# Values of the attention: the product with the probabilities taken once for four query blocks instead of once for two

## The chip, the cores and the metric

The kernel runs on one core of one Trainium2 chip. The metric is the device time of one execution in microseconds (us), lower is better. A core has a matrix engine (TensorE, PE in the profile, with its weight loads on a row of their own, PEld), a vector engine (VectorE, DVE), a scalar engine (ScalarE, ACT), a general engine (GpSimd, POOL) and an engine that issues transfers (SyncE, SP). Each works off a queue of its own in order; semaphores tie them together. A matrix product takes a stationary operand of 128x128 (loaded just ahead of it) and streams the columns of a moving operand past it; the result lands in an accumulation bank (PSUM) of 128 rows by 512 columns.

## The reference, cut to what matters

One layer of a streaming encoder on 1024 frames of 1024 channels: a normalised input goes through one wide projection, then attention beside a pooling branch, a gated mix, and a gated feed-forward part. The change lies in the attention alone, 8 heads of 64 channels; chunk c of 64 frames sees its own chunk and the eight before it:

```python
sc = jnp.einsum('bqhd,bkhd->bhqk', q_c, k_c) * scale + bias
sc = jnp.where(valid, sc, -1e30)
p = jax.nn.softmax(sc, axis=-1)
return jnp.einsum('bhqk,bkhd->bqhd', p, v_c)
```

## The kernel before, in words

The program is one core's instruction stream in four stages: input projection with its normalisation and pooling, attention (the stage of this change), output and mix, feed-forward. All matrix products except transposes are in a rounded 32-bit format (fp32r in the profile). Where precision asks for it, an operand is held as two such tensors, the rounded value and the rest ("hi" and "lo"); `split` (L77) makes the pair from a source: ACT casts to hi, DVE (or POOL) subtracts to get lo.

Attention works in blocks of 128 queries by 128 keys; there are 8 query blocks, and query block j sees key blocks j-4 to j, where they exist. A loop over 32 steps (head h, J) handles two query blocks, 2J and 2J+1, in each step. The parts of a step, each emitted in a later turn of the loop than the one before:

- `scores` (L836): for each of the two query blocks the products of queries and keys into a bank pair `pst` (640 columns once all five key blocks exist, as two products of 320, each for the hi and lo part of the keys), then on DVE bias and row maximum (L864), on ACT the exponential (L866), on DVE the reciprocal (L868), on POOL the scaling (L870) to the probabilities `pe`.
- `transposed` (L874): PE turns each 128x128 block of `pe` (L891) into one of two banks `tp`; ACT and DVE split it (L78) into `pth` and `ptl`. There are two pairs of these tiles, for even and odd J, each with 6 slots of key blocks by 256 columns, the two query blocks side by side. For J of 2 and 3 a step has ten blocks, in three fillings of a bank: 4, 2 and 4.
- `values_of` (L905): for each slot two products (hi, lo) of 256 columns (L916) with the values `vv` of one key block stationary, summed in one half of a bank `f`. The first slot holds nothing for the second query block and the last nothing for the first; those blocks of `pth` and `ptl` are zeros, set once by POOL (L962, L963). A head takes 4, 8, 12 and 12 products. After the odd J, `f` holds four query blocks: ACT and DVE add its two halves (L924, L925), and a split writes a piece of `ath` and `atl`.
- `yb_units` (L929): products of the pooling branch with its output weights (`ybp`, 512 columns each), handed out in 32 pieces of six products, by the table `NU`, one entry for each turn of the loop; they give PE something to do while the other engines are at work. After every second piece DVE multiplies the bank by a gate `sgb` (L944).

In turn i of the loop (L968), the order of emission is: scores of step i, transposes of step i-1, the `yb` pieces, values of step i-2. A scheduler then places the instructions on the engines, mostly near that order, with those that would wait put later. `tp` and `pst` have two buffers each, `f` has one bank, and `yb` has one.

Of the kernel before, what the change touches and what calls it, by code (L numbers as in the profile page):

```python
# [10 lines left out]
F32 = mybir.dt.float32  # L11
F32R = mybir.dt.float32r
# [5 lines left out]
P = 128  # L18
# [27 lines left out]
def trunk(ctx, tc, xn, xt, w_first, w_in, cols, gain_pre, bias, w_ao, w_pg, w_po, w_o, gains, w_up, w_dn, out):  # L46
    nc = tc.nc
    A, V, G = nc.scalar, nc.vector, nc.gpsimd
# [28 lines left out]
    def split(hi, lo, src, eng=None):  # L77
        return A.copy(hi, src), (eng or V).tensor_tensor(lo, src, hi.bitcast(F32), ALU.subtract)  # L78
# [287 lines left out]
    with ExitStack() as ph:  # L366
# [30 lines left out]
        for n, tag in enumerate(("T1h", "T1l", "T2h", "T2l")):  # L397
# [6 lines left out]
        q = {(i, j): raw_tile(f"xq{i}{j}").rearrange("p (k n) -> p k n", k=4)  # L404
             for j in range(2) for i in range(2)}
# [371 lines left out]
    ap_ = pool(atp, "atp", 1, side="right")  # L777
    ath = ap_.tile([P, 4, S], F32R, name="ath")
    atl = ap_.tile([P, 4, S], F32R, name="atl")

    wrp = pool(atp, "wrp", 2, side="right")

# [25 lines left out]
    with ExitStack() as ph:  # L808
# [64 lines left out]

        def transposed(J, pes):  # L874

            pth, ptl = PT[J % 2]
            fl = [t.rearrange("p s q -> p (s q)") for t in (pth, ptl)]
            (pa, na), (pb, nb) = pes
            sa, sb = 5 - na, 6 - nb
            if J == 0:  # L880
                banks = [[(pa, 0, 1, sa, 0), (pb, 0, 2, sb, 1)]]
            elif J == 1:
                banks = [[(pa, 0, 3, sa, 0)], [(pb, 0, 4, sb, 1)]]
            else:
                banks = [[(pa, 1, 4, 1, 0)], [(pa, 0, 1, 0, 0), (pb, 0, 1, 1, 1)], [(pb, 1, 4, 2, 1)]]
            for runs in banks:
                tp = psT.tile([P, 512], F32, tag="t", name="tp")
                c = 0
                for pe, b0, n, s0, a in runs:
                    for b in range(b0, b0 + n):  # L890
                        nc.tensor.transpose(tp[:, c * P:(c + 1) * P], pe[:, b * P:(b + 1) * P], ident)  # L891
                        c += 1
                if J >= 2 and len(runs) == 2:
                    moves = [(0, 2, [t[:, 0:768].rearrange("p (b q) -> p b q", b=2)[:, :, :P] for t in fl])]
                else:
                    moves, c = [], 0
                    for pe, b0, n, s0, a in runs:
                        moves.append((c, n, [t[:, s0:s0 + n, a * P:(a + 1) * P] for t in (pth, ptl)]))
                        c += n
                for c, n, (hi, lo) in moves:  # L900
                    split(hi, lo, tp[:, c * P:(c + n) * P].rearrange("p (b q) -> p b q", b=n))

        avs = {}

        def values_of(h, J):  # L905
            m, e = h // 2, h % 2
            vv = vvs[m]
            if J % 2 == 0:
                avs[h] = psf.tile([P, 512], F32, tag="f", name="f")
            f = avs[h]  # L910
            slots = [s for s in range(6) if 2 * J - 4 + s >= 0]
            fo = f[:, 256 * (J % 2):256 * (J % 2) + 256]
            for s in slots:
                kb = 2 * J - 4 + s
                for x, t in enumerate(PT[J % 2]):
                    nc.tensor.matmul(fo, vv[:, kb, e].rearrange("p a d -> p (a d)"),  # L916
                                     t[:, s], start=s == slots[0] and x == 0,
                                     stop=s == slots[-1] and x == 1)
            if J % 2 == 0:
                return  # L920
            r = slice(64 * e, 64 * e + 64)
# [32 lines left out]
        load_pair(0)  # L954
        load_yb(1)
        load_wy(2)
        PT = []
        for i in range(2):
            pth = atn.tile([P, 6, 256], F32R, name=f"pth{i}", bufs=1)
            ptl = atn.tile([P, 6, 256], F32R, name=f"ptl{i}", bufs=1)  # L960
            for t in (pth, ptl):
                G.memset(t[:, 0, 128:256].bitcast(F32), 0.0)  # L962
                G.memset(t[:, 5, 0:128].bitcast(F32), 0.0)  # L963
            PT.append((pth, ptl))
        units = yb_units()
        NU = [2, 2, 0, 1, 0, 1, 1, 2] + [0, 1, 1, 2] * 5 + [0, 1, 1, 1, 1, 1]
        steps = [(h, J) for h in range(H) for J in range(4)]
        for i in range(len(steps) + 2):  # L968
            if 0 < i < len(steps):
# [590 lines left out]
```

## Time and profile before

| what | value |
| --- | --- |
| median of 3 runs (1236.58 to 1236.9) | 1236.82 us |
| span of the profiled execution, first to last instruction | 1234.9 us |
| PE busy, share of the span | 1225.3 us, 99% |
| DVE busy | 949.6 us, 77% |
| ACT busy | 667.2 us, 54% |
| POOL busy | 211.0 us, 17% |
| granted PE clock, mean of the core | 0.998 |

The profiled execution has no time of its own besides its span; the span is 1.9 us under the median of the runs. A busy engine is one that has an instruction in flight. Matmuls overlap, so the duration of one in a row (389 ns for 512 columns) is longer than what it costs in a stream of them; the distance from one start to the next is what counts.

### The profile page before, as it was taken

How to read it: one execution, taken by the hardware profiler on the slowest of the kernel's cores; microseconds unless marked ns; L12 is line 12 of the kernel's file. 1: busy time of each engine (PE TensorE's matmuls, PEld its weight loads, DVE VectorE, ACT ScalarE, POOL GpSimd, SP SyncE). 2: the span in 40 equal slices, each digit the busy share in tenths (PEclk: the TensorE clock that was granted, in tenths of full speed). 3: DMA queues.
4: the chain of work that ended last, by engine and by line, in shares of the span. 5: the costliest groups of instructions: out<-in, count | busy, mean ns of one | idle time of the engine just before them, and what ended most of it. 6: DMA issues, size and time to landing. Idle time of an engine off the chain costs nothing.

```text
span 1234.9 us, 16242 instructions
## 1 busy us (share of the span) xinstructions
PE 1225.3 (99%) x5743; PEld 1020.9 (83%) x5743; DVE 949.6 (77%) x1551; ACT 667.2 (54%) x1171; POOL 211.0 (17%) x183
## 2 busy tenths in 40 slices
PE   9999999999999999999999999999999999999997
PEld 7888888888889987888888888888888888888886
DVE  5898677866788878756799887667666675999968
ACT  6764355555577773434546555554545455445553
POOL 0000000043254545000000112433333300000000
PEclk9999999999999999999999999999999999999999
DMA  9879245438886845322352232222132127902103
GB/s 329 333 256 350 85 147 207 154 124 264 291 276 214 264 178 207 137 86 76 113 196 111 111 145 103 71 84 102 52 102 85 61 68 255 350 18 103 34 1 137
DMA packets 63857, 193.84 MB, mean 157 GB/s; under 512 B 6048, under 2 KB 6688, under 8 KB 58656
## 3 DMA queue, kind: packets, MB, share of 16 engines
q1 hardware_dynamic: 55712, 176.55, 40.8%
q10 hardware_dynamic: 7056, 12.59, 2.7%
q0 software_dynamic: 1008, 3.67, 0.7%
q8 instruction: 45, 0.74, 0.2%
q14 instruction: 36, 0.29, 0.1%
HBM read 139.84 MB, written 52.95 MB: 156 GB/s over the span
## 4 chain that ended last, share of the span: by engine, by line
PE 92%; DVE 6%; issue 1%; DMA 0%; ACT 0%; POOL 0%; DVEq 0%; ACTq 0%
PE X_u L84 19%; PE X_i L84 12%; PE Y_u L84 10%; PE Y_i L84 9%; PE X L84 7%; PE wops L1115 7%; PE Z_u L84 4%; PE y L84 4%; PE ybp L84 4%; PE Y L84 4%; PE f L916 3%; PE tp L891 2%; PE Z_i L84 2%; PE first L466 2%; PE pst L848 1%; DVE a L1405 1%
## 5 line engine op out<-in xcount | busy, mean ns | idle before, releaser
L1239 DVE SCALAR_TENSOR_TENSOR hc<-hu,cv,hc 128x1022 f32<-128x1022 f32 (+1 forms) x88 | 115.6, 1315 | 27.7 <-ACT hc L1234 27.7
L78 ACT CAST wh_u<-s_u 128x512 fp32r<-128x512 f32 x88 | 54.4, 619 | 90.2 <-PE Y_u L84 47.7
L78 DVE TENSOR_TENSOR wl_u<-s_u,wh_u 128x512 fp32r<-128x512 f32 x88 | 62.4, 711 | 33.9 <-ACT wh_u L78 33.9
L78 ACT CAST wh_i<-s_i 128x512 fp32r<-128x512 f32 x64 | 39.8, 622 | 75.9 <-PE X_i L84 36.0
L78 ACT CAST wh_u<-wup 128x512 fp32r<-128x512 f32 x60 | 37.3, 621 | 52.0 <-PE X_u L84 27.5
L78 DVE TENSOR_TENSOR wl_i<-s_i,wh_i 128x512 fp32r<-128x512 f32 x64 | 46.2, 722 | 21.3 <-ACT wh_i L78 16.3
L1234 ACT ACTIVATE hc<-hu,cv 128x1024 f32<-128x1024 f32 x44 | 54.6, 1244 | 9.8 <-DVE hu L1183 8.9
L202 POOL TENSOR_TENSOR s_i<-win 128x512 f32<-128x512 f32 x4 | 5.9, 1481 | 257.0 <-DVE wl_i L78 246.6
L202 POOL TENSOR_TENSOR s_u<-wup 128x512 f32<-128x512 f32 x15 | 25.7, 1713 | 139.4 <-DVE wl_u L78 139.4
L78 DVE TENSOR_TENSOR ptl<-tp,pth 128x512 fp32r<-128x512 f32 (+3 forms) x80 | 42.8, 552 | 7.7 <-ACT pth L78 7.2
L866 ACT ACTIVATE pe<-sm,st 128x640 f32<-128x640 f32 (+2 forms) x64 | 44.3, 695 | 7.7 <-DVE st L864 7.5
L870 POOL TENSOR_SCALAR pe<-pe,st 128x640 f32<-128x640 f32 (+4 forms) x58 | 40.7, 705 | 44.2 <-DVE st L868 30.0
L78 ACT CAST pth<-tp 128x512 fp32r<-128x512 f32 (+3 forms) x80 | 36.3, 474 | 15.9 <-PE tp L891 11.0
L78 DVE TENSOR_TENSOR wl_u<-wup,wh_u 128x512 fp32r<-128x512 f32 x60 | 43.0, 719 | 1.2 <-ACT wh_u L78 0.5
L84 PE MATMUL ybp<-mx,wh_yb 128*128 128x512 f32 x128 | 43.3, 412 | 0.0
L1244 ACT ACTIVATE hc<-hc 128x1024 f32<-128x1024 f32 x22 | 23.4, 1062 | 36.9 <-DVE hc L1239 36.9
L864 DVE CUSTOM_DVE_ANT_0 sm<-pst,bt 128x640 f32<-128x640 f32 (+2 forms) x64 | 40.7, 651 | 3.0 <-issue 1.7
L206 POOL TENSOR_TENSOR s_u<-s_u,wup 128x512 f32<-128x512 f32 x15 | 19.4, 1291 | 102.3 <-DVE wl_u L78 99.6
L916 PE MATMUL f<-pth,vv 128*128 128x256 f32 x144 | 36.6, 286 | 0.0
L916 PE MATMUL f<-ptl,vv 128*128 128x256 f32 x144 | 36.5, 287 | 0.0
L208 POOL TENSOR_TENSOR s_u<-wup 128x512 f32<-128x512 f32 x15 | 32.2, 2144 | 23.5 <-DVE wl_u L78 23.5
L891 PE MATMUL tp<-ident,pe 128*128 128x128 f32 x240 | 35.3, 274 | 0.2
(523 smaller groups left out, 4135.7 us busy)
## 6 DMA issues: line engine op xcount, KB each, us to landing
wup<-in_w_up SPq DMA_DIRECT2D x22, 1024.0 KB, 5.0
win<-in_w_in SPq DMA_DIRECT2D x16, 1024.0 KB, 7.0
g_d<-hc SPq DMA_DIRECT2D x20, 512.0 KB, 2.6
sig_d<-d ACTq DMA_DIRECT2D x32, 256.0 KB, 2.0
a<-g_d SPq DMA_DIRECT2D x8, 1024.0 KB, 11.4
b<-in_w_dn SPq DMA_DIRECT2D x8, 1024.0 KB, 12.7
w<-in_w_in SPq DMA_DIRECT2D x12, 512.0 KB, 7.3
x<-in_xn SPq DMA_DIRECT2D x8, 512.0 KB, 8.5
```

The costliest lines, as they stand in the source:

```text
L78: return A.copy(hi, src), (eng or V).tensor_tensor(lo, src, hi.bitcast(F32), ALU.subtract)
L84: nc.tensor.matmul(ps, a[i], b[i], start=start and i == 0 and p == 0, stop=stop and i == n - 1 and p == 2, skip_group_check=True,)
L202: self.eng.tensor_tensor(self.s1, self.w21, self.w22, ALU.add)
L208: self.eng.tensor_tensor(self.s3, self.w11, self.w21, ALU.subtract)
L864: V.tensor_tensor_reduce(so, sv, bv, -1.0, 3e38, ALU.add, ALU.min, st[:, 0:1])
L866: A.activation(pe[:, :n], sm[:, :n], AF.Exp, scale=-1.0, bias=st[:, 0:1], accum_out=st[:, 1:2])
L870: (V if 4 * h + J in (0, 1, 31) else G).tensor_scalar(pe[:, :n], pe[:, :n], st[:, 2:3], 1.0, ALU.mult, ALU.mult)
L891: nc.tensor.transpose(tp[:, c * P:(c + 1) * P], pe[:, b * P:(b + 1) * P], ident)
L916: nc.tensor.matmul(fo, vv[:, kb, e].rearrange("p a d -> p (a d)"), t[:, s], start=s == slots[0] and x == 0, stop=s == slots[-1] and x == 1)
L1115: nc.tensor.matmul(ps[:, 512 * c:512 * c + 512], a[k // 4][:, k % 4, sl], wo[k][b][:, 512 * c:512 * c + 512], start=k == 0 and x == 0, sto ...
L1234: A.activation(c, hu, AF.Identity, scale=cv[:, C_CW + 88 + b:C_CW + 89 + b], bias=cv[:, C_CB + b:C_CB + b + 1])
L1239: V.scalar_tensor_tensor(c[:, n:], hu[:, :S - n], cv[:, w:w + 1], c[:, n:], ALU.mult, ALU.add)
```

## The change

The two pairs of tiles become one pair of 20 blocks of 128x128: block 5a+d holds query block a of the group of four, and key block a+d-4 counted from the group's first. An even J fills a of 0 and 1, an odd J a of 2 and 3. Blocks of one key block then lie four blocks apart, and a product takes all query blocks that see a key block, one to four of them, as a moving operand in pieces of 128 columns at that distance. Values are taken only after an odd J: 8 products after J=1 (widths 512, 384, 256 and 128 columns, hi and lo) and 16 after J=3 (each width four times), with the widest first. No zero blocks are left. In the loop, the group's values come ahead of the next step's transposes, after that turn's `yb` pieces, and `NU` hands these out one in each turn. A tile `edge` of 8 columns is placed behind `ath` and `atl` and set to zero by POOL; nothing reads it. The splits of the transposed blocks have the same count and sizes as before and write contiguous blocks.

```diff
@@ -777,6 +777,8 @@
     ath = ap_.tile([P, 4, S], F32R, name="ath")
     atl = ap_.tile([P, 4, S], F32R, name="atl")
+    edge = ap_.tile([P, 8], F32, name="edge")
+    G.memset(edge, 0.0)
...
@@ transposed @@
-            pth, ptl = PT[J % 2]
-            fl = [t.rearrange("p s q -> p (s q)") for t in (pth, ptl)]
+            k = 2 * (J % 2)
             (pa, na), (pb, nb) = pes
-            sa, sb = 5 - na, 6 - nb
+            spans = [(pa, 0, na, k, 5 - na), (pb, 0, nb, k + 1, 5 - nb)]
...
-                banks = [[(pa, 1, 4, 1, 0)], [(pa, 0, 1, 0, 0), (pb, 0, 1, 1, 1)], [(pb, 1, 4, 2, 1)]]
+                banks = [[(pa, 0, 4, k, 0)], [(pa, 4, 1, k, 4), (pb, 0, 1, k + 1, 0)], [(pb, 1, 4, k + 1, 1)]]
...
+                    at = 5 * a + d
+                    split(PT[0][:, at:at + n], PT[1][:, at:at + n],
+                          tp[:, c * P:(c + n) * P].rearrange("p (b q) -> p b q", b=n))
+                    c += n
@@ values_of @@
-            slots = [s for s in range(6) if 2 * J - 4 + s >= 0]
-            fo = f[:, 256 * (J % 2):256 * (J % 2) + 256]
-            for s in slots:
-                kb = 2 * J - 4 + s
-                for x, t in enumerate(PT[J % 2]):
-                    nc.tensor.matmul(fo, vv[:, kb, e].rearrange("p a d -> p (a d)"),
-                                     t[:, s], start=s == slots[0] and x == 0,
-                                     stop=s == slots[-1] and x == 1)
             if J % 2 == 0:
                 return
+            f = psf.tile([P, 512], F32, tag="f", name="f")
+            grid = [t.rearrange("p (a d) q -> p a d q", a=4) for t in PT]
+            slots = (4, 5, 6, 7) if J == 1 else (3, 4, 2, 5, 1, 6, 0, 7)
+            for s in slots:
+                kb = 2 * J - 6 + s
+                a0, a1 = max(0, s - 4), min(3, s)
+                for x, t in enumerate(grid):
+                    flat = t.rearrange("p a d q -> p (a d) q")
+                    at = 5 * a0 + s - a0
+                    nc.tensor.matmul(f[:, a0 * P:(a1 + 1) * P], vv[:, kb, e].rearrange("p a d -> p (a d)"),
+                                     flat[:, at:at + 4 * (a1 - a0) + 1:4],
+                                     start=s == slots[0] and x == 0, stop=s == slots[-1] and x == 1,
+                                     skip_group_check=True)
@@ -954,16 +954,9 @@
-            for t in (pth, ptl):
-                G.memset(t[:, 0, 128:256].bitcast(F32), 0.0)
-                G.memset(t[:, 5, 0:128].bitcast(F32), 0.0)
-            PT.append((pth, ptl))
+        PT = [atn.tile([P, 20, P], F32R, name=f"pt{x}", bufs=1) for x in "hl"]
         units = yb_units()
-        NU = [2, 2, 0, 1, 0, 1, 1, 2] + [0, 1, 1, 2] * 5 + [0, 1, 1, 1, 1, 1]
+        NU = [2, 2, 0, 1, 1, 1, 1, 1] + [1, 1, 1, 1] * 5 + [1, 1, 1, 1, 1, 1]
...
+            if i >= 2 and steps[i - 2][1] % 2:
+                for _ in range(NU[i]):
+                    next(units, None)
+                values_of(*steps[i - 2])
+                NU[i] = 0
             if 1 <= i <= len(steps):
                 transposed(steps[i - 1][1], pend.pop(i - 1))
...
-            if i >= 2:
-                values_of(*steps[i - 2])
```

What the scheduler makes of it shows on two engines. The first place is PE's queue in the middle of the stage, at the values of head 3 after J=1 (f is their bank, tp a bank of transposes, ybp a piece of the pooling branch, pth and ptl the hi and lo blocks). Before:

```order
L84 MATMUL ybp_3837<-mx09_2114,wl_yb3_3662 128x512
L916 MATMUL f_3844<-pth1_3034,vv1_3212 128x256
L916 MATMUL f_3844<-ptl1_3035,vv1_3212 128x256
L916 MATMUL f_3844<-pth1_3034,vv1_3212 128x256
L916 MATMUL f_3844<-ptl1_3035,vv1_3212 128x256
L916 MATMUL f_3844<-pth1_3034,vv1_3212 128x256
L891 MATMUL tp_3885<-ident_77,pe_3820 128x128 x4
L916 MATMUL f_3844<-ptl1_3035,vv1_3212 128x256
```

and in the changed kernel:

```order
L84 MATMUL ybp_3840<-mx05_1595,wl_yb4_3837 128x512
L917 MATMUL f_3847<-ptl_3031,vv1_3200 128x512
L917 MATMUL f_3847<-pth_3030,vv1_3200 128x384
L917 MATMUL f_3847<-ptl_3031,vv1_3200 128x384
L917 MATMUL f_3847<-pth_3030,vv1_3200 128x256
L917 MATMUL f_3847<-ptl_3031,vv1_3200 128x256
L917 MATMUL f_3847<-pth_3030,vv1_3200 128x128
L917 MATMUL f_3847<-ptl_3031,vv1_3200 128x128
L892 MATMUL tp_3861<-ident_77,pe_3771 128x128 x4
```

The products have become fewer and of four widths, and the next step's transposes, which stood among them, now stand behind the group.

The second place is ACT's queue at the turn from one head to the next: casts of transposed blocks, exponentials (ACTIVATE), and COPY, the first step of emptying the bank `f`. Before:

```order
L78 CAST pth_3034<-tp 128x4x128 [waits PE_49,Activation_49]
L866 ACTIVATE pe,st<-sm,st 128x384 [waits DVE_49]
L866 ACTIVATE pe,st<-sm,st 128x512 [waits DVE_49]
L78 CAST pth_3028<-tp 128x128 [waits PE_49,Activation_49]
L78 CAST pth_3028<-tp 128x2x128 [waits DVE_49]
L924 COPY sm_4035<-f 64x512 [waits PE_49]
```

and in the changed kernel:

```order
L78 CAST pth<-tp 128x512 [waits PE_49,Activation_49]
L868 ACTIVATE pe,st<-sm,st 128x512 [waits DVE_49,Activation_49]
L78 CAST pth<-tp 128x128 [waits PE_49]
L868 ACTIVATE pe,st<-sm,st 128x640 [waits DVE_49]
L78 CAST pth<-tp 128x256 [waits DVE_49,PE_49]
L924 COPY sm_3978<-f 64x512 [waits PE_49]
```

The casts of the next head's first blocks (128 and 256 columns) went from the other pair of tiles (`pth_3028`, while the values in progress read `pth_3034`) to the one pair that these values read, and the wider of the two waits for PE as well.

More of the change, by code (lines that the diff above doesn't have):

```diff
@@ L874, in transposed @@
         def transposed(J, pes):
-            pth, ptl = PT[J % 2]
-            fl = [t.rearrange("p s q -> p (s q)") for t in (pth, ptl)]
+            k = 2 * (J % 2)
             (pa, na), (pb, nb) = pes
-            sa, sb = 5 - na, 6 - nb
+            spans = [(pa, 0, na, k, 5 - na), (pb, 0, nb, k + 1, 5 - nb)]
             if J == 0:
-                banks = [[(pa, 0, 1, sa, 0), (pb, 0, 2, sb, 1)]]
+                banks = [spans]
             elif J == 1:
-                banks = [[(pa, 0, 3, sa, 0)], [(pb, 0, 4, sb, 1)]]
+                banks = [spans[:1], spans[1:]]
             else:
-                banks = [[(pa, 1, 4, 1, 0)], [(pa, 0, 1, 0, 0), (pb, 0, 1, 1, 1)], [(pb, 1, 4, 2, 1)]]
+                banks = [[(pa, 0, 4, k, 0)], [(pa, 4, 1, k, 4), (pb, 0, 1, k + 1, 0)], [(pb, 1, 4, k + 1, 1)]]
             for runs in banks:
@@ L888, in transposed @@
                 c = 0
-                for pe, b0, n, s0, a in runs:
+                for pe, b0, n, a, d in runs:
                     for b in range(b0, b0 + n):
@@ L892, in transposed @@
                         c += 1
+                c = 0
                 if J >= 2 and len(runs) == 2:
[L894 to L901, printed above, removed]
@@ L903, in trunk @@
-        avs = {}
+                    runs = [(None, 4, 2, k, 4)]
+                for pe, b0, n, a, d in runs:
+                    at = 5 * a + d
+                    split(PT[0][:, at:at + n], PT[1][:, at:at + n],
+                          tp[:, c * P:(c + n) * P].rearrange("p (b q) -> p b q", b=n))
+                    c += n
         def values_of(h, J):
             m, e = h // 2, h % 2
[L907 to L910, printed above, removed]
-            slots = [s for s in range(6) if 2 * J - 4 + s >= 0]
-            fo = f[:, 256 * (J % 2):256 * (J % 2) + 256]
-            for s in slots:
-                kb = 2 * J - 4 + s
-                for x, t in enumerate(PT[J % 2]):
-                    nc.tensor.matmul(fo, vv[:, kb, e].rearrange("p a d -> p (a d)"),
-                                     t[:, s], start=s == slots[0] and x == 0,
-                                     stop=s == slots[-1] and x == 1)
@@ L919, in values_of @@
             if J % 2 == 0:
                 return
+            vv = vvs[m]
+            f = psf.tile([P, 512], F32, tag="f", name="f")
[11 more added lines that the diff above has]
+                                     skip_group_check=True)
@@ L956, in trunk @@
         load_wy(2)
[L957 to L960, printed above, removed]
-            for t in (pth, ptl):
-                G.memset(t[:, 0, 128:256].bitcast(F32), 0.0)
-                G.memset(t[:, 5, 0:128].bitcast(F32), 0.0)
-            PT.append((pth, ptl))
+        PT = [atn.tile([P, 20, P], F32R, name=f"pt{x}", bufs=1) for x in "hl"]
         units = yb_units()
-        NU = [2, 2, 0, 1, 0, 1, 1, 2] + [0, 1, 1, 2] * 5 + [0, 1, 1, 1, 1, 1]
+        NU = [2, 2, 0, 1, 1, 1, 1, 1] + [1, 1, 1, 1] * 5 + [1, 1, 1, 1, 1, 1]
         steps = [(h, J) for h in range(H) for J in range(4)]
```

## The prediction

> **What bounds the kernel now.** I read the page first, then the share of engines in the stretch of the attention, then its groups of instructions, and last its timeline on PE, where the distance between starts gives the price of a product. The page:
>
> ```profile
> span 1234.9 us, 16242 instructions
> PE 1225.3 (99%) x5743; PEld 1020.9 (83%) x5743; DVE 949.6 (77%) x1551; ACT 667.2 (54%) x1171; POOL 211.0 (17%) x183
> PE 92%; DVE 6%; issue 1%; DMA 0%; ACT 0%; POOL 0%; DVEq 0%; ACTq 0%
> ```
>
> PE is busy for 99% of the span, and the chain that ended last lies on PE for 92%. So PE work that goes is time that goes, unless a wait takes its place. The stage, by the table of stretches, from the first scores to the last values:
>
> ```profile
> core 0: us, PE busy (x) PEld busy (x) DVE busy (x) ACT busy (x) POOL busy (x), PEclk, DMA share, GB/s
> 322.00:460.00 138.00, 137.76 (x920) 123.70 (x919) 114.38 (x319) 102.42 (x249) 66.74 (x86) 1.00 0.71 234
> ```
>
> PE is never idle there and its clock is full (1.00), but DVE has 23.6 us left of 138, ACT 35.6: the other engines follow closely. The groups on PE:
>
> ```profile
> L84 PE MATMUL ybp<-mx,wh_yb 128*128 128x512 f32 x128 | 43.3, 412 | 0.0
> L916 PE MATMUL f<-pth,vv 128*128 128x256 f32 x144 | 36.6, 286 | 0.0
> L916 PE MATMUL f<-ptl,vv 128*128 128x256 f32 x144 | 36.5, 287 | 0.0
> L891 PE MATMUL tp<-ident,pe 128*128 128x128 f32 x240 | 35.3, 274 | 0.2
> L848 PE MATMUL pst<-qk 128*128 128x320 f32 x64 | 19.1, 310 | 0.0
> ```
>
> The values are 288 products. Their mean of 286 ns is a duration with overlap, not a price. The price is on the timeline (start, duration):
>
> ```profile
> 321.88 0.28 PE L857 MATMUL pst<-qk 128*128 128x256 f32 x1
> ...
> 402.18 0.28 PE L916 MATMUL f<-pth,vv 128*128 128x256 f32 x1
> 402.30 0.60 PE L891 MATMUL tp<-ident,pe 128*128 128x128 f32 x4
> 402.66 0.37 PE L916 MATMUL f<-ptl,vv 128*128 128x256 f32 x1
> 402.86 0.28 PE L916 MATMUL f<-pth,vv 128*128 128x256 f32 x1
> ...
> 406.96 0.34 PE L857 MATMUL pst<-qk 128*128 128x384 f32 x1
> 407.13 0.34 PE L857 MATMUL pst<-kl,qk 128*128 128x384 f32 x1
> 407.31 0.39 PE L857 MATMUL pst<-qk 128*128 128x512 f32 x1
> 407.54 0.40 PE L857 MATMUL pst<-kl,qk 128*128 128x512 f32 x1
> 407.78 0.40 PE L84 MATMUL ybp<-mx,wh_yb 128*128 128x512 f32 x1
> ...
> 409.93 0.28 PE L916 MATMUL f<-pth,vv 128*128 128x256 f32 x1
> ...
> 411.32 0.31 PE L848 MATMUL pst<-qk 128*128 128x320 f32 x1
> 411.47 0.31 PE L848 MATMUL pst<-kl,qk 128*128 128x320 f32 x1
> ...
> 460.13 0.28 PE L916 MATMUL f<-ptl,vv 128*128 128x256 f32 x1
> ```
>
> Twelve products of 256 columns fill 409.93 to 411.32: 0.116 us each. 384 columns cost (407.31 - 406.96) / 2 = 0.175, 512 columns (407.78 - 407.31) / 2 = 0.235, 320 columns 0.15. Each step of 128 columns is worth about 0.059 ((0.235 - 0.116) / 2). Four transposes stand between two value products: 402.86 - 402.18 = 0.68, less two value products of 0.116, leaves 0.45, so 0.112 us for a transpose of 128 columns, almost the price of 256 columns.
>
> **The products.** Removed: 288 x 0.116 = 33.4 us. Added, for each head 3 slots of each width (one after J=1, two after J=3), hi and lo, 8 heads: 48 products each of 512, 384, 256 and 128 columns. The first three widths have rows: 48 x (0.235 + 0.175 + 0.116) = 25.2 us. The 128-column product in fp32r has none; nothing in this kernel multiplies fp32r narrower than 256. Call its price X. Then the change is 25.2 + 48 X - 33.4, zero at X = 0.171.
>
> From below: by the slope of the wider ones, 0.116 - 0.059 = 0.057. From above I take the row with four times the columns, 0.235. In between lies the row nearest in kind, the transpose: 128 columns streamed after a fresh stationary operand of 128x128, 0.112. I take 0.112, since a value product too loads a new operand every time, and something other than columns plainly holds the transpose up. That makes 48 x 0.112 = 5.4, in all 30.6 us, a gain of 2.8 us. With the ends: 27.9 (gain 5.5) and 36.5 (loss 3.1).
>
> The Trainium skill has both readings on one page, "TensorE: Matmul & The Clock Gate". In its section "Back-to-back issue gap" an isolated product costs its columns at 2.4 GHz plus 2.5 ns, 56 ns for 128 columns; by that the gain is an estimated 5.5 us. In "LDWEIGHTS (loading the stationary operand)" the load takes the operand's columns at 1.2 GHz, 107 ns for 128; by that it is an estimated 3.1. The transpose row, 0.112, agrees with the second.
>
> **The moving operand in pieces** of 128 columns, four blocks apart: no row shows such a reading, every moving operand so far is contiguous. I price it at nothing; if the jumps cost, they add to 144 wide products, and 20 ns each would eat the gain.
>
> **Transposes and splits.** 240 transposes and 80 pairs of cast and subtraction stay, in the same sizes, writing contiguous blocks instead of blocks 256 apart. Rows of before, with other work of the two engines:
>
> ```profile
> L78 DVE TENSOR_TENSOR ptl<-tp,pth 128x512 fp32r<-128x512 f32 x40 | 27.5, 688 | 4.7 <-ACT pth L78 4.2
> L866 ACT ACTIVATE pe<-sm,st 128x640 f32<-128x640 f32 x32 | 26.5, 831 | 5.4 <-DVE st L864 5.3
> L78 ACT CAST pth<-tp 128x512 fp32r<-128x512 f32 x40 | 23.1, 577 | 10.0 <-PE tp L891 9.9
> L78 DVE TENSOR_TENSOR ptl<-tp,pth 128x256 fp32r<-128x256 f32 x24 | 10.0, 417 | 2.6 <-ACT pth L78 2.6
> L78 ACT CAST pth<-tp 128x256 fp32r<-128x256 f32 x24 | 8.9, 373 | 5.2 <-DVE ptl L78 4.7 <-PE tp L891 0.6
> L944 DVE TENSOR_TENSOR sgb<-ybp,sgb 128x512 f32<-128x512 f32 x16 | 11.0, 685 | 0.5 <-PE ybp L84 0.3
> ```
>
> No change on DVE and ACT; their 23.6 and 35.6 us of room cover a small one either way.
>
> **Zero blocks and `edge`.** Eight fills go from POOL, one small one comes:
>
> ```profile
> 323.07 0.22 POOL L962 MEMSET pth<- 128x128 f32 x1
> 332.27 0.80 POOL L870 TENSOR_SCALAR pe<-pe,st 128x640 f32<-128x640 f32 x1 [6.97 <-DVE st L868]
> ```
>
> POOL waits 6.97 us for DVE afterwards, so nothing is won. `edge` moves what lies behind it by 32 bytes; nothing in the trace puts a price on an address, I take zero.
>
> **The single pair of tiles.** The casts of the next head's first blocks now wait for the running group, and behind them in ACT's queue stand an exponential, the next cast and the COPY that empties `f`; DVE's subtractions follow, and PE's next transposes need the bank that these free. But the slots are taken in the order 3, 4, 2, 5, 1, 6, 0, 7: the first blocks to be overwritten (a=0 with d=4, a=1 with d=3 and 4) are read by slots 4 and 5, done after half the group. Behind slot 5's hi product PE still has 0.175 + 4 x 0.116 + 4 x 0.112 and, by the order, two scores products of 0.15 and three transposes, 1.7 us in all, against one cast of 256 columns and one subtraction, 0.373 + 0.417 = 0.79. Covered; 0.
>
> **`yb` pieces.** The same 32, one per turn instead of 0, 1, 1, 2. Before, PE waited about once a head for a bank of transposes:
>
> ```profile
> 400.37 0.40 PE L84 MATMUL ybp<-mx,wl_yb 128*128 128x512 f32 x1
> 400.76 0.41 PE L891 MATMUL tp<-ident,pe 128*128 128x128 f32 x2
> ...
> PEld tp L891 <- issue: 2.8, 7, 0.4
> PEld tp L891 <- DVE ptl L78: 1.7, 6, 0.4
> ```
>
> Here 0.39 us lie between the starts where 0.235 do without a wait: 0.155 lost. The queue behind it is the same kind of sequence in the changed kernel, a subtraction that stands behind `sgb` (0.685) on DVE. I leave the waits as they are. After the attention the order on every engine is the same as before, so nothing else moves.
>
> Sum: -2.8 us. The span of 1234.9 becomes 1232.1; the runs' median lies 1.9 above the span, and I add that unchanged: 1236.8 - 2.8 = **1234.0 us**. A measurement of this kernel can tell about 0.2%, 2.5 us, from no change; the forecast stands just past it.
>
> **Rivals.**
>
> *The narrow products are slow.* Below 256 columns the rounded format could lose its rate, so that 128 columns cost as much as 512. For it: no such product exists in this kernel, and scores of one key block (128 columns) are computed 256 wide. Against it: the transpose's 0.112, though that is another mode. Price X = 0.235, 48 x (0.235 - 0.112) = 5.9 us more than forecast: 1239.9, slower by 3.1. It decides from X = 0.171 on.
>
> *Narrow products cost their columns.* X = 0.057: 48 x 0.055 = 2.6 us better, 1231.3. Against it the transposes. [...]
>
> *The gain is taken back as waits.* DVE keeps its 114.38 us while PE's 138 shrink, and the group of values now comes in one piece with the splits of its last bank just ahead. Two more waits of 0.155 a head are 16 x 0.155 = 2.5 us: 1236.5, no change. For it: DVE's share; against it: the order puts other products between the last transposes of a group and the products that need them.
>
> *The one pair of tiles holds the next head up.* If the casts are released only by the group's last product, PE has 0.63 us of cover (two scores products, three transposes) against cast, exponential, cast and subtraction, 0.25 + 0.831 + 0.373 + 0.417 = 1.87 (the 128-column cast, 0.25, is an estimate by the step from 512 to 256 columns): 1.24 a head, 7 turns, 8.7 us: 1242.7. It decides when the casts are released later than slot 5.
>
> **How the numbers follow.** Forecast 0.46, slow narrow products 0.25, cheap ones 0.10, waits 0.14, tiles 0.05. The forecast's own range is 1232.8 to 1235.5 (X from 0.09 to 0.14); two thirds of it lie past 0.2%. Faster: 0.31 + 0.10 = 0.41. Same: 0.15 + 0.14 + 0.05 of the slow products, which stand near their bound too, = 0.34. Slower: 0.20 + 0.05 = 0.25. The range reaches from the cheap to the slow narrow product, 1231.0 to 1240.2, and leaves out the tiles and the tails.
>
> **What would show it.** The starts of the 128-column products on the timeline: 0.11 apart (forecast), 0.06 or 0.24. 512, 384 and 256 columns at 0.235, 0.175 and 0.116 in spite of the pieces. The attention, now 321.88 to 460.13 at its last value product, ending near 457.3. Waits of weight loads for the transposes no longer than now. The forecast is wrong if a 128-column product costs over 0.17, if wide ones in pieces cost more than contiguous ones, or if the casts of the next head's first blocks show waits on PE that PE itself then waits out.

## The result, and the profile after

The changed kernel takes 1242.41 us (1239.8 to 1242.84), the kernel before 1236.9 (1236.58 to 1237.02): ratio 1.0042, 95% interval 1.0031 to 1.0053. It is slower by 5.5 us. The profiled execution took 1242.84 us, its span is 1241.1, 6.2 us above that of before.

The page of the changed kernel, with the span, the engines and the chain that ended last:

```profile
span 1241.1 us, 16085 instructions
PE 1226.8 (99%) x5647; PEld 1016.2 (82%) x5647; DVE 951.5 (77%) x1551; ACT 669.7 (54%) x1171; POOL 208.9 (17%) x176
PE 90%; DVE 8%; issue 1%; ACT 0%; DMA 0%; POOL 0%; DVEq 0%
```

It reads like the page before: 96 matmuls fewer, PE still 99% busy, and only DVE's 8% of the chain instead of 6% says that something waits longer. The products themselves did what they were meant to. The timeline of PE, at a group of values after J=1:

```profile
452.01 0.39 PE L917 MATMUL f<-ptl,vv 128*128 128x512 f32 x1
452.24 0.34 PE L917 MATMUL f<-pth,vv 128*128 128x384 f32 x1
...
452.59 0.28 PE L917 MATMUL f<-pth,vv 128*128 128x256 f32 x1
452.71 0.28 PE L917 MATMUL f<-ptl,vv 128*128 128x256 f32 x1
452.83 0.22 PE L917 MATMUL f<-pth,vv 128*128 128x128 f32 x1
452.89 0.27 PE L917 MATMUL f<-ptl,vv 128*128 128x128 f32 x1
453.00 0.92 PE L892 MATMUL tp<-ident,pe 128*128 128x128 f32 x6
```

From start to start: 0.23 us for 512 columns, 0.175 for 384 (two of them in 0.35), 0.12 for 256, in spite of the pieces; 0.06 for the first product of 128 columns and 0.11 for the next. After J=3, where four stand in a row, it is 0.06, then three times 0.11. So 48 of them cost some 4.6 us and all the value products 29.9 instead of 33.4: 3.5 us less work on TensorE. The time went up all the same: this gain got lost in the attention, and more was lost behind it.

**In the attention** the 3.5 us didn't come out. The table of stretches:

```profile
322.00:460.00 138.00, 136.30 (x817) 117.09 (x816) 114.40 (x317) 103.69 (x247) 64.34 (x79) 1.00 0.81 246
```

The stretch is 138 us long in both kernels, so 136.30 us busy against 137.76 say that TensorE's visible idle time grew by 1.46 us; in the place of the value products stand 9 `y` products more, from the stage behind. Not all idle time is visible: a product's record lasts longer than the distance to the next start (0.28 us at 0.116), so that a gap of up to 0.16 us behind a product does not show. What a head costs is better read from the same product in two heads, four heads apart. In before and in the changed kernel:

```profile
373.21 0.34 PE L857 MATMUL pst<-qk 128*128 128x384 f32 x1
440.89 0.34 PE L857 MATMUL pst<-qk 128*128 128x384 f32 x1
```

```profile
374.03 0.33 PE L859 MATMUL pst<-qk 128*128 128x384 f32 x1
441.09 0.34 PE L859 MATMUL pst<-qk 128*128 128x384 f32 x1
```

16.92 us a head became 16.77. The products' gain alone would have made it 16.5 (3.5 / 8 = 0.44 less). The view of waits (us, times, longest) shows what stands in the place of the rest:

```profile
PEld ybp L84 <- DVE sgb L944: 3.0, 9, 0.4
PEld tp L892 <- DVE ptl L78: 1.8, 4, 1.0
PEld f L917 <- ACT pth L78: 1.1, 5, 0.3
```

The first wait is new: the first product of a `yb` pair waits until VectorE has emptied the one `yb` bank of the pair before. The second is about what it was (1.7 us before), the third was 0.3.

**Behind the attention** 5.9 us are lost at one product. It is the first of the fifth `y` tile; in before:

```profile
480.43 0.39 PE L84 MATMUL y<-ath,wl_ya 128*128 128x512 f32 x1
480.84 0.47 PE L84 MATMUL y<-ath,wh_ya 128*128 128x512 f32 x1
```

and in the changed kernel:

```profile
481.18 0.40 PE L84 MATMUL y<-ath,wl_ya 128*128 128x512 f32 x1
484.88 0.76 PE L84 MATMUL y<-ath,wh_ya 128*128 128x512 f32 x1 [3.30 <-DVE ya L1030]
485.44 0.63 PE L84 MATMUL y<-atl,wh_ya 128*128 128x512 f32 x1
...
490.56 0.41 PE L84 MATMUL y<-atl,wh_ya 128*128 128x512 f32 x1
...
480.00:490.00 10.00, 6.70 (x19) 5.02 (x18) 9.25 (x8) 2.57 (x5) 4.73 (x3) 0.69 0.48 169
```

Up to the row at 481.18 the changed kernel is 0.75 us late, 0.45 of them already at the first scores product (322.33 against 321.88), behind a stage that the change leaves alone. Then 3.70 us pass where before 0.41 did: 3.29 lost. Then 13 products start 0.43 apart instead of 0.234, and the clock granted in those ten microseconds is 0.69: (490.56 - 484.88) - 13 x 0.234 = 2.6 lost. Together 6.7 us; 0.5 of them come back further on, which leaves the 6.2 of the span. The half rate did not strike every time: four of the five executions of this kernel show a granted clock of 0.996 or 0.997 and take 1242.3 to 1242.84 us, the fifth shows 0.998 and takes 1239.8.

Why VectorE answers late there is on its own timeline. Two tiles hold `y`, so the fifth needs the third emptied (L1030 here, L1034 in before). Before:

```profile
461.11 0.69 DVE L925 TENSOR_TENSOR sm<-f,sm 64x512 f32<-64x512 f32 x1 [1.86 <-ACT sm L924]
463.99 1.23 DVE L1034 TENSOR_TENSOR ya<-y,ya 128x1024 f32<-128x1024 f32 x1 [0.82 <-PE y L84]
...
479.48 1.21 DVE L1034 TENSOR_TENSOR ya<-y,ya 128x1024 f32<-128x1024 f32 x1
```

and in the changed kernel, with GpSimd's second pair of subtractions below it:

```profile
465.19 0.69 DVE L925 TENSOR_TENSOR sm<-f,sm 64x512 f32<-64x512 f32 x1 [2.80 <-ACT sm L924]
468.08 1.23 DVE L1030 TENSOR_TENSOR ya<-y,ya 128x1024 f32<-128x1024 f32 x1 [0.82 <-PE y L84]
...
471.17 1.21 DVE L1030 TENSOR_TENSOR ya<-y,ya 128x1024 f32<-128x1024 f32 x1
...
475.70 3.42 DVE L1031 TENSOR_TENSOR ya<-ya 128x1024 f32<-128x1024 f32 x1
479.80 2.13 DVE L78 TENSOR_TENSOR mix00l<-ya,mix00h 128x512 fp32r<-128x512 f32 x1 [0.69 <-ACT mix00h L78]
...
483.52 1.21 DVE L1030 TENSOR_TENSOR ya<-y,ya 128x1024 f32<-128x1024 f32 x1
484.77 1.23 DVE L1031 TENSOR_TENSOR ya<-ya 128x1024 f32<-128x1024 f32 x1
```

```profile
475.18 6.20 POOL L78 TENSOR_TENSOR wol<-wo,woh 128x1024 fp32r<-128x1024 f32 x2
```

The whole chain stands 4.1 us later (468.08 against 463.99). It starts from the last value product, which was at 460.13 and is at 464.21 now. In PE's queue 23 `y` products stand ahead of it, 9 before, and 14 x 0.234 = 3.3 us, which with the 0.75 us of lateness makes up the shift; the bank `f` is emptied behind it. From the first to the third L1030 the chain is as long as before, 15.4 us (483.52 - 468.08) against 15.5, although VectorE takes the second tile's L1030 (471.17) ahead of the first tile's `mix` subtractions now, and took it behind them before: what has changed is its start. In before the third tile was emptied at 480.69 (479.48 + 1.21), and the product that needs it started 0.15 later, as it does in the changed kernel (484.73 and 484.88). It stood 0.41 us behind its predecessor there, not 0.234: the place was waiting by some 0.18 us already, and there was no slack to take. And the chain is slow because VectorE's operations are stretched while GpSimd subtracts: L1031 takes 3.42 us at 475.70 and 1.23 at 484.77.

### The profile page after: what moved, and what is told of

Same layout as the page of the kernel before. It is cut to its first block, busy times and chain, and to the rows that moved or that the text cites. A ratio compares the mean times of both kernels' runs of the same rounds, so it can differ in the third digit from the quotient of the medians.

```text
span 1241.1 us, 16085 instructions
## 1 busy us (share of the span) xinstructions
PE 1226.8 (99%) x5647; PEld 1016.2 (82%) x5647; DVE 951.5 (77%) x1551; ACT 669.7 (54%) x1171; POOL 208.9 (17%) x176
## 4 chain that ended last, share of the span: by engine, by line
PE 90%; DVE 8%; issue 1%; ACT 0%; DMA 0%; POOL 0%; DVEq 0%
PE X_u L84 19%; PE X_i L84 12%; PE Y_u L84 10%; PE Y_i L84 9%; PE X L84 7%; PE wops L1111 7%; PE Z_u L84 4%; PE Y L84 3%; PE ybp L84 3%; PE y L84 3%; PE f L917 2%; PE tp L892 2%; PE Z_i L84 2%; PE first L466 2%; PE pst L850 1%; DVE a L1401 1%
## 5 line engine op out<-in xcount | busy, mean ns | idle before, releaser
L78 DVE TENSOR_TENSOR wl_i<-s_i,wh_i 128x512 fp32r<-128x512 f32 x64 | 44.9, 702 | 22.0 <-ACT wh_i L78 16.9
L892 PEld LDWEIGHTS tp<-ident,pe 128*128 128x128 f32 x240 | 28.2, 140 | 8.3 <-DVE ptl L78 1.8
L84 PE MATMUL Y_u<-T1h,wl_u 128*128 128x512 f32 x88 | 34.2, 389 | 0.0
```

The source lines that it names most:

```text
L84: nc.tensor.matmul(ps, a[i], b[i], start=start and i == 0 and p == 0, stop=stop and i == n - 1 and p == 2, skip_group_check=True,)
```

## The experiments

The runs below are compared with the kernel before on the same chip, 1236.6 to 1236.9 us. Where an expectation speaks of the third `y` tile that waits, it is the third that is emptied late and the fifth that waits for it.

**Without the subtractions for the low half of w_o** in `split_wo`'s calls behind the third and fifth `y` tile:

```
             if m in (2, 4):
-                split_wo(wraw[m // 2 - 1], wopa, G)
+                raw = wraw[m // 2 - 1]
+                for k in range(2):
+                    hi = wopa.tile([P, D], F32R, tag="woh", name="woh")
+                    A.copy(hi, raw[:, k * D:(k + 1) * D])
+                    wo.append((hi, hi))
```

> The changed kernel without POOL's four subtractions of the first half of w_o, right behind the attention (the hi part stands in for the lo part of that half, so half of one small correction of the mix product is left out). Nothing else moves. Theory A (the loss lies behind the attention: the last value product comes 4.1 us later, so DVE's gating chain starts 4.1 us later, runs slowly while POOL subtracts, and PE waits 3.3 us for the third bank of y and then runs 5.3 us at half clock): the gating of 475.70 takes about 1.2 us instead of 3.42, the wait falls under 0.5 us, the clock stays full, 1242.4 - 3.3 - 2.5 = 1236.6 us. Rival B (the chain is late on its own, POOL's work beside it does not matter): a wait of over 2 us and the half clock stay, 1241 us or more.

Measured: 1236.13 us, ratio 0.9995 (0.9987 to 1.0004). The 6.3 us are back. The chain still starts late, at 467.53, but reaches the third L1030 9.2 us later (476.73) instead of 15.4, and the fifth tile's first product no longer waits:

```profile
480.63 0.39 PE L84 MATMUL y<-ath,wl_ya 128*128 128x512 f32 x1
480.86 0.40 PE L84 MATMUL y<-ath,wh_ya 128*128 128x512 f32 x1
```

The same edit in the kernel before:

> The kernel before, with GpSimd's four subtractions for the first half of w_o left out (the high half is used in the place of the low one, so the last projection's result is less exact). Theory A, the subtractions cost the changed kernel 6.3 us only because its gating chain starts 4.1 us late and the third y tile then waits for VectorE: before, the same place waited 0.16 us, so this run gives 1236.7, no more than 0.3 below the kernel before. Rival, the subtractions cost either kernel their time: 1230.6, as much below the kernel before as the first experiment lay below the changed kernel.

Measured: 1235.95 us, ratio 0.9992 (0.9983 to 1.0001), 0.8 less than before, where the expectation allowed 0.3, and not the 6.3 of the changed kernel. So the subtractions have little price of their own: they cost 6 us only on top of the late chain. And with them away the two kernels stand at 1235.95 and 1236.13: the attention of the changed kernel has brought nothing.

The other way to part the two engines, with nothing left out, hands the same subtractions to VectorE, three tiles later in the program (the scheduler then ran two of the four at 468.99 and 472.94, between VectorE's work for the first two tiles):

```
-            if m in (2, 4):
-                split_wo(wraw[m // 2 - 1], wopa, G)
+            if m in (5, 7):
+                split_wo(wraw[m // 2 - 2], wopa, V)
```

> The changed kernel, whole, with the four subtractions on VectorE, behind the sixth and the eighth y tile, instead of on GpSimd behind the third and the fifth. Theory A, it is the two engines' working at once that stretches VectorE's gating chain: 1236 to 1236.8, as without the subtractions. Rival, VectorE has no room for 4 x 1.2 us of them in that stage: 1238 or more, with waits of y products for VectorE further back.

Measured: 1236.17 us, ratio 0.9994 (0.9985 to 1.0002). VectorE's timeline there:

```profile
470.68 1.21 DVE L1031 TENSOR_TENSOR ya<-ya 128x1024 f32<-128x1024 f32 x1
...
474.08 0.68 DVE L78 TENSOR_TENSOR mix00l<-ya,mix00h 128x512 fp32r<-128x512 f32 x1
...
476.42 1.21 DVE L1030 TENSOR_TENSOR ya<-y,ya 128x1024 f32<-128x1024 f32 x1
```

VectorE has four subtractions more, and still empties the third `y` tile 7 us earlier (476.42 against 483.52), since L1031 takes 1.21 us and the `mix` subtractions 0.68 instead of up to 2.13. The Trainium skill's page "SBUF — State Buffer", section "Who interferes with whom", says that a VectorE instruction with two SBUF inputs contends with a GpSimd instruction that reads SBUF, and that one blocks the other; the rows agree, for L1031 and the `mix` subtractions read two SBUF tiles, while L1030, which reads one of its two inputs from the bank, keeps its 1.21 to 1.23 us throughout.

**The pieces of `yb` at other steps.** Later, `NU = [2, 2, 0, 0] + [1] * 30`:

> The changed kernel with the pieces of the pooling branch handed out one turn later (table 2, 2, 0, 0, then 1 in each turn), so that a pair of pieces ends in an odd turn, ahead of the values, and the next pair starts behind the transposes. Theory C (the pair that ends in an even turn is followed too closely by the next one, which waits for DVE to empty the one bank: 0.24 us, nine times, 3.0 us of waits of weight loads): those waits fall under 1 us, a head's period goes from 16.75 to 16.5 us, and the last values come 2 us earlier or more, so that part of the wait behind the attention goes too: 1235 to 1240 us. Rival D (waits only change places, DVE's share sets the period): the period stays at 16.7 or more and the time within 0.6 us of 1242.4.

Measured: 1239.1 us, ratio 1.0021 (1.0012 to 1.0031). Earlier, `NU = [2, 2, 1, 1, 1, 1, 1, 1] + ...`:

> As the run before, with the same distance between the pairs, but handed out one turn earlier (2, 2, then 1 in each turn), so that the pieces end two turns earlier at the end of the attention. Theory C: the period falls to 16.5 us here too, but the end of the attention has less to put between the last transposes, so the last value product gains less than in the run before: 1236 to 1241 us, not faster than the run before. Rival D: no change against 1242.4.

Measured: 1241.03 us, ratio 1.0033 (1.0020 to 1.0046); the profiled execution of this one was the shortest of its runs, 1239.48. The wait for the `yb` bank is gone in both, but in the run with later pieces the others have grown (1.8 and 1.1 before the edit):

```profile
PEld tp L892 <- DVE ptl L78: 4.5, 14, 0.9
PEld f L917 <- ACT pth L78: 2.7, 9, 0.5
```

A head takes 17.1 us with the later pieces and 16.9 with the earlier ones, where theory C had 16.5 and rival D 16.7 or more. So C's mechanism is missed, though its time for the first run is met; D's time is missed there. What they win against the changed kernel comes from the fifth `y` tile, which waits less, and from the clock: 18 and 21 `y` products stand ahead of the last value product instead of 23, and the third L1030 starts at 482.00 and 482.73 instead of 483.52. Later pieces:

```profile
483.36 0.48 PE L84 MATMUL y<-ath,wh_ya 128*128 128x512 f32 x1 [2.10 <-DVE ya L1030]
483.67 0.40 PE L84 MATMUL y<-atl,wh_ya 128*128 128x512 f32 x1
```

Earlier pieces:

```profile
484.08 0.47 PE L84 MATMUL y<-ath,wh_ya 128*128 128x512 f32 x1 [2.90 <-DVE ya L1030]
484.40 0.39 PE L84 MATMUL y<-atl,wh_ya 128*128 128x512 f32 x1
```

After 2.10 and 2.90 us without work the next products run at full rate; after 3.30 they ran at half. With earlier pieces this holds for the two executions of 1239.48 and 1239.57 us, which show a clock of 0.998; the other three show 0.996 or 0.997 and take 1241.03 to 1242.45.

The old table, 0, 1, 1, 2, without the subtractions:

> The changed kernel with the old table of yb pieces (0, 1, 1, 2 in a head) and, as in the first experiment, without the four subtractions, so that the attention shows by itself; that one gave 1236.13. Theory W1, the waits that ate the products' gain belong to the new table (the next pair's first product behind VectorE's emptying of the one yb bank, 2.8 us): 1233.4 to 1234. Theory W2, VectorE's answers come late in every order, and the waits only change their name: 1235.5 to 1236.8, with waits of the transposes or of the value products in the place of those for the yb bank.

Measured: 1236.9 us, ratio 0.9999 (0.9990 to 1.0008), 0.8 more than with the new table. W1 falls: the waits only change their names.

```profile
PEld f L917 <- ACT pth L78: 2.6, 11, 0.3
PEld tp L892 <- DVE ptl L78: 2.6, 8, 0.6
```

**The narrow products alone**, in the kernel before:

```
-            slots = [s for s in range(6) if 2 * J - 4 + s >= 0]
+            slots = [s for s in (1, 2, 3, 4, 0, 5) if 2 * J - 4 + s >= 0]
...
+                q = slice(128 * (s == 5), 256 - 128 * (s == 0))
...
-                    nc.tensor.matmul(fo, vv[:, kb, e].rearrange("p a d -> p (a d)"),
-                                     t[:, s], start=s == slots[0] and x == 0,
+                    nc.tensor.matmul(fo[:, q], vv[:, kb, e].rearrange("p a d -> p (a d)"),
+                                     t[:, s, q], start=s == slots[0] and x == 0,
```

> The kernel before, in which only the products with the first and the last key block are made 128 columns wide instead of 256 with a block of zeros (96 of 288 products; the slots with both query blocks come first; the zero blocks and their fills go). Two pairs of tiles, the values of each step and the pieces stay. Theory E (a narrow product costs about 0.09 us on the mean, as the changed kernel's trace has it, and what PE saves here is time): 96 x (0.116 - 0.09) = 2.5 us, 1234.4 us. Rival F (narrow products are slow): slower than 1236.9. Rival G (what PE saves goes into waits within the attention): within 0.8 us of 1236.9.

Measured: 1241.98 us, ratio 1.0042 (1.0029 to 1.0055). The expectation of a gain is missed, though the products are as cheap as in the changed kernel:

```profile
393.50 0.22 PE L917 MATMUL f<-pth,vv 128*128 128x128 f32 x1
393.56 0.28 PE L917 MATMUL f<-ptl,vv 128*128 128x128 f32 x1
393.67 0.27 PE L917 MATMUL f<-pth,vv 128*128 128x128 f32 x1
...
PEld f L917 <- DVE sm L926: 3.3, 8, 0.5
```

A new wait stands at the first value product of each head, for the one bank `f` to be emptied, and a head takes 17.5 us instead of 16.9. The scheduler sorted PE's queue anew for the shorter products and the other order of slots, so this run tells that cheap products do not make a fast stage, and not what they would be worth in the old order.

**What holds the attention's pace?** First a link of it made short, VectorE's multiplication by the gate at the `yb` bank (the changed kernel without the subtractions of w_o; the three runs behind it leave them out too):

```
-                            V.tensor_tensor(sg[:, s], ps, sg[:, s], ALU.mult)
+                            V.tensor_tensor(sg[:, s][:, :64], ps[:, :64], sg[:, s][:, :64], ALU.mult)
```

> The changed kernel without the four subtractions, and with VectorE's multiplication of each yb bank by its gate cut from 512 columns to 64 (the other columns of that gate are left out of the result). It takes some 0.55 us from each of 16 instructions, 8.8 us from VectorE in the attention. Theories W1 and W2, VectorE's answers are what TensorE waits for there: the waits for the yb bank (2.8 us) go and those of the transposes shrink, 1232.5 to 1233.8. Rival P, VectorE is not what holds the stage (TensorE, a transfer or the scores' chain through ScalarE): 1235.8 to 1236.4.

Measured: 1236.76 us, ratio 0.9999 (0.9990 to 1.0008), even 0.6 above 1236.13. The rival comes out for this link, though above its range, and W1 and W2 as stated there fall: the wait for the `yb` bank shrinks from 2.8 us to 0.6, and nothing is won. (The theory P of the next two runs is another: that TensorE itself is waited for.)

Then TensorE's own work cut, in the changed kernel and, for comparison, in the kernel before:

```
-                for x, t in enumerate(grid):
+                for x, t in enumerate(grid[:1] if s in (2, 5) else grid):
```

> The changed kernel without the four subtractions and without the low half's value products of three slots a head (384 columns each, 3 x 0.175 x 8 = 4.2 us less on TensorE; the result is less exact by these). Theory P, TensorE is what the attention waits for, and the products' gain was lost to waits of this one order: 1236.1 - 4.2 = 1231.9. Theory H, the hand-over of transposes (bank, cast, subtraction, bank free again) sets the stage's pace, and TensorE's work is no longer what it waits for: 1235 to 1236.5, the missing products' time standing as waits of weight loads for the subtractions and casts.

```
-                for x, t in enumerate(PT[J % 2]):
+                for x, t in enumerate(PT[J % 2][:1] if J > 1 and s in (2, 3) else PT[J % 2]):
```

> The kernel before without the four subtractions and without the low half's value products of two slots in the third and fourth step of a head (32 x 0.116 = 3.7 us less on TensorE, the result less exact). It stands beside 1235.95, the kernel before without the subtractions. Theory P: 1232.2. Theory H, if the hand-over already set the pace before: 1235 to 1236.2.

Measured: 1235.03 (ratio 0.9986, 0.9977 to 0.9995) and 1235.19 (0.9986, 0.9978 to 0.9995). Of 4.2 us taken off TensorE 1.1 come out (1236.13 - 1235.03), of 3.7 in the kernel before 0.8 (1235.95 - 1235.19). P falls, for both kernels, in so far as it says that time taken off TensorE comes out. The rest stands as waits; in the kernel before with fewer products transposes now wait for GpSimd's scaling of the probabilities:

```profile
PEld tp L891 <- POOL pe L870: 2.9, 6, 1.0
```

Then VectorE's subtraction for the probabilities' low half, cut to a quarter:

```
-                    split(PT[0][:, at:at + n], PT[1][:, at:at + n],
-                          tp[:, c * P:(c + n) * P].rearrange("p (b q) -> p b q", b=n))
+                    src = tp[:, c * P:(c + n) * P].rearrange("p (b q) -> p b q", b=n)
+                    A.copy(PT[0][:, at:at + n], src)
+                    V.tensor_tensor(PT[1][:, at:at + n, :32], src[:, :, :32],
+                                    PT[0][:, at:at + n, :32].bitcast(F32), ALU.subtract)
```

> The changed kernel without the four subtractions, and with VectorE's subtraction for the probabilities' low half cut to 32 columns of each 128 (the others stay zero; the result is less exact). A bank of transposes comes free some 0.5 us earlier, and VectorE has some 30 us less to do; TensorE's instructions stay. Theory H: the waits of transposes for the subtraction and of value products for what stands behind it shrink, 1232.5 to 1234. Theory P and any other holder (the scores' chain through ScalarE and GpSimd, a transfer): 1235.5 to 1236.5.

Measured: 1233.52 us, ratio 0.9974 (0.9964 to 0.9984): 2.6 us come out with TensorE's instructions unchanged. A head takes 16.51 us ((438.29 - 372.25) / 4), near the 16.5 that the products' gain alone asks for:

```profile
372.25 0.42 PE L859 MATMUL pst<-qk 128*128 128x384 f32 x1
438.29 0.42 PE L859 MATMUL pst<-qk 128*128 128x384 f32 x1
```

So in the changed kernel the time per head hangs more on VectorE's part in the hand-over of probabilities (bank, cast, subtraction) than on TensorE's products. The edit also takes 20 us of 114 off VectorE in this stage; the short gate took 6 off and won nothing, but no run tells the shorter link from the lighter engine for good.

Four more runs keep the whole computation, with the subtractions of w_o on VectorE (1236.17). A third bank for transposes, the one of the values' results in its idle steps:

```
-            for runs in banks:
-                tp = psT.tile([P, 512], F32, tag="t", name="tp")
+            for x, runs in enumerate(banks):
+                third = J % 2 and x == 0
+                tp = (psf if third else psT).tile([P, 512], F32, tag="f" if third else "t", name="tp")
```

> The changed kernel, whole, with the four subtractions on VectorE as in the eighth run (1236.17), and with the first bank of transposes of a head's second and fourth step taken from the bank of the values' results, which is empty then, so that three banks hold transposes there. Theory H2, the number of banks sets the pace: the waits of transposes for the subtraction go, 1233 to 1234.5. Rival H1, the time that ScalarE and VectorE take for a bank sets it: 1235.7 to 1236.6, the waits moving to value products or scores.

and the same with the later pieces:

> The changed kernel, whole, with the four subtractions on VectorE, the third bank and the yb pieces as late as in the second run (none in the first head's third and fourth step, then one a step to the end). There the waits of transposes for the subtraction were 4.5 us and of value products for the cast 2.7; H2: most of the 4.5 goes, 1232 to 1234. H1: 1236 to 1237.

Measured: 1237.58 (ratio 1.0008, 0.9999 to 1.0017) and 1235.7 (0.9993, 0.9984 to 1.0002). In the second, the transposes' wait for the subtraction went from 4.5 us to 0.9, as H2 would have it, but the next link stands in its place:

```profile
PEld tp L893 <- POOL pe L872: 4.3, 7, 0.9
PEld tp L893 <- DVE ptl L78: 0.9, 4, 0.2
```

The first lies above both theories. The time of the second is too high for H2 and a little too low for H1. It has the lowest median of the versions that compute everything, yet its interval reaches to no change.

The value products handed out in two halves, the second behind the next step's transposes, and this together with the third bank:

```
-                values_of(*steps[i - 2])
+                second = values_of(*steps[i - 2])
+                next(second)
...
                 transposed(steps[i - 1][1], pend.pop(i - 1))
+            for _ in second:
+                pass
```

> The changed kernel, whole, with the four subtractions on VectorE, and with the value products of a group handed out in two halves, the first four slots ahead of the next step's transposes, the others behind them. Theory L, the value products in one run leave the banks of transposes without work between them: 1234 to 1235.5. Rival, the place of the products doesn't matter: 1235.7 to 1236.6.

> The changed kernel, whole, with the four subtractions on VectorE, the third bank and the values in two halves. If banks and place both count, 1232.5 to 1234; if neither, 1235.7 to 1236.6; if one alone, as that run.

Measured: 1244.89 (ratio 1.0067, 1.0055 to 1.0080) and 1239.69 (1.0026, 1.0016 to 1.0037). Neither theory had the first, and the second fits none of its three cases: the place does matter, but this one is worse. In the first a head takes 18.5 us, and transposes wait 6.9 us for GpSimd's scaling:

```profile
PEld tp L892 <- POOL pe L872: 6.9, 6, 1.3
```

**Without the 32-byte tile:**

> The changed kernel without the 32-byte tile behind the result's tiles; nothing else is changed. All theories: 1242.4, as the changed kernel. Rival, the address of what lies behind it has a price: another time by 1 us or more.

Measured: 1242.62 us, ratio 1.0047 (1.0034 to 1.0060), 0.2 from the changed kernel. The tile has no price.

## Why the prediction was wrong

**The products** were priced rightly in kind. X was taken at 0.112; the runs show 0.06 for the first and 0.11 for each that follows, some 0.095 in the mean, and a gain of 3.5 us of TensorE work where 2.8 were forecast. The rival of slow narrow products fell: none costs over 0.12. Of the two readings of the Trainium skill's page in the prediction each has its place: 56 ns fits the first of a run, 107 ns those behind it.

**The pieces four blocks apart, the zero blocks and `edge`** cost nothing, as taken (0.23, 0.175, 0.12; the run without `edge`).

**The single pair of tiles** is covered, as worked out, by the trace alone; no run put the second pair back. In the whole stage ACT's casts wait for a value product once, at 345.10, and TensorE goes on meanwhile:

```profile
ACT pth L78 <- PE f L917: 0.9, 1, 0.9
```

The time of the rival that has this pair hold the next head up, 1242.7 us, lies next to the measured 1242.41, but that is chance: it charges for casts held up in seven turns, and the view has one.

**"So PE work that goes is time that goes, unless a wait takes its place"** is the step that failed first. It was read from PE's 99% and from 137.76 us busy of 138. TensorE was full: by the prediction's own prices a head of before holds 36 value products, 30 transposes, 24 `yb` products and 24 of scores, an estimate of 16.86 us in the 16.92 that it takes. But that only says that a head can't be shorter with this work; the next limit stood right behind, at least in the orders that the scheduler made. The two runs with fewer products show that only a quarter of TensorE's time comes out, before the change too (0.8 of 3.7 us). The Trainium skill's page "Perfetto Trace Analysis", section "Identifying the Most-Contended Engine", says that the busy time of matmuls is not a good measure of how close TensorE is to its limit. The trace agrees in part: in the changed kernel some 16.42 us of products (16.86 - 0.44) stand in a head of 16.77, 98%, while the records show 99% busy; in before both say 99% or more.

**"I leave the waits as they are"** failed with it. The `yb` bank alone shows 3.0 us of new waits. The rival that took the gain back as waits had the mechanism (two more waits a head, no change, 1236.5), and this is what the attention by itself did, with about one longer wait a head (nine, 0.33 us in the mean, instead of 0.155): 1236.13 without the disturbance behind it. Its reason, VectorE's share of busy time, is borne out in part: 20 us less of VectorE's subtractions gave 2.6 us, but less of its gate multiplication gave none.

**"After the attention the order on every engine is the same as before, so nothing else moves"** is the step that made the sign wrong. The program's text behind the attention was the same; the order on the engines was not. The scheduler put 14 more `y` products ahead of the last value product, so that VectorE's chain starts 4.1 us later, while the fifth `y` tile's turn on TensorE came only 0.75 us later; and VectorE takes the second tile's L1030 ahead of the first tile's `mix` subtractions. In the trace of before the fifth `y` tile's first product started 0.41 us behind its predecessor instead of 0.234, so its bank came free with no slack at all, and this was there to be read. The shift cost 3.3 us of waiting and, in four of five executions, 2.6 of half rate; the runs without the subtractions, in both kernels, and with the subtractions on VectorE show it.

**Left open:** what the scheduler's reason was to put the `y` products there; which link of the hand-over sets a head's pace, and how much of it the scheduler's order makes. Each edit was sorted anew, and each wait removed came back under another name. No run kept the order and changed one duration alone.

## What to carry to other kernels

A full engine tells how short a stage can't become with its work; it does not tell that the time follows when the work shrinks. Here some 16.9 us of products filled a head of 16.92, and 0.46 us less of them a head gave 0.1 in the time. Before a saving is forecast in full, ask how far behind the next chain stands; an experiment that cuts the same engine's work in the kernel before shows it. Where a change can reorder the end of one stage, follow the first chain of the next stage to the first place where a buffer comes free just when it is needed: there the missing slack cost more than the products saved. A long wait on TensorE can be paid twice, the second time in clock: here a wait of 3.30 us drew 2.6 us more in most executions.

## What the runs showed of the hardware

- In a run of products of 128 columns in fp32r the second starts 0.06 us after the first, and each one behind it 0.11 later, like the transposes. Moving operands in pieces of 128 columns, four blocks apart, cost nothing more.
- After an idle time of 3.30 us TensorE ran at half rate for 5.7 us, in the run without `edge` after 3.24; in the profiled executions after 2.10 and 2.90 it did not. In the changed kernel the granted clock is 1.00 up to 483 us, 0.87 from 483 to 484 and 0.50 from 484 on, so it fell some 2.2 us after the last product's record ended (481.58). The Trainium skill's page "TensorE: Matmul & The Clock Gate", section "What's actually happening", gives a window of about 3.4 us that runs freely, so that the moment of the change varies. The executions agree that it varies: with the same kernel some fell to half rate and some did not. An idle time of 3.4 us was not needed here.
- VectorE operations with two SBUF inputs take up to 3.42 us instead of 1.23 while GpSimd subtracts from SBUF.
